# Once-used experts without room go on in the list for both halves: 29 + 46 + 29 tiles instead of 30 + 47 + 30

## Chip, cores and metric

The kernel runs on 1 core of one Trainium2 chip. The metric is the device time of one execution, in microseconds; a time of a kernel is the median of its runs.

## The reference, cut to what matters

One layer of a hybrid decoder trunk over 256 tokens of width 2048: a mixing part (window attention and a linear recurrence) and then PEER, a retrieval of experts by product keys. Each token takes, for each of 8 heads, the best 16 of 16,384 experts; an expert is a row of a table U and a row of a table V.

```python
s = einsum('chpd,hpkd->chpk', q, sub_keys)         # two sets of 128 key scores per head
top_s, top_i = top_k(s, 16)
cand = top_s[:, :, 0, :, None] + top_s[:, :, 1, None, :]
best_s, best_c = top_k(cand.reshape(128, 8, 256), 16)
experts = i1 * 128 + i2                            # the keys of the best 16 sums
g = softmax(best_s)
act = gelu(einsum('chkd,cd->chk', u_tab[experts], x))
out = einsum('chkd,chk->cd', v_tab[experts], g * act)
```

The output is the residual plus this sum, normalised, for 256 tokens. They are worked on in two halves of 128 tokens.

## The kernel before, in words

**Mixing, up to about 500 us.** Blocks of weights of 128 output columns come in on SyncE's queue (`load`), are split into a high and a low float32r part by ScalarE (`hi`, line 115) and VectorE (`lo`, line 117), and are multiplied with high and low parts of the activations. `items` holds all these half blocks of the first stages in one list. The loop at the end goes through them: it loads and splits block i + 1, calls block i's function, and then whatever `at` has hung on slot i.

**U, up to about 1160 us.** All 128 blocks of 128 experts of U are multiplied with all 256 tokens (`add_pair`, lines 133 and 134), so that every expert's activation for every token is known, and these are written to a table in HBM, `wg_d`, with one row of 4 x 128 numbers per expert: activations of half 0, gates of half 0, gates of half 1, activations of half 1. Beside this stage runs `routing`, a generator that `pump` advances by about 1200 ns of VectorE work per slot, always behind the `lo` of the next block. It finds the top keys and experts, has GpSimd scatter the gates into `wg_d` (256 scatters, line 701), and then calls `lists`.

**The lists.** For each half, an expert is used not at all, by one token or by several. `lists` counts this with one-hot matmuls and sorts the experts of the first 126 key columns into six classes: S0 and S1 (used by one token of this half alone), M0 and M1 (by several tokens of this half alone), DO (by one token of each half), BO (by both halves otherwise). Three lists of places are filled, each from both ends: S0 from the front and M0 from the back, DO and BO, S1 and M1. `CAPS` gives the tiles of 128 places of each class, `BASES` their first tile, `NT` their sum. Classes of one list share its room: `fits` says whether an expert's number plus those of the other end is under the room (lines 766 and 767), or under the class's cap (line 769); `cum` becomes the place. Experts that fit nowhere are counted (`many`, lines 775 and 776), summed over partitions by a matmul (line 778) and put in `nov`. At the end 128 one-hot matmuls (line 801) turn the places into a list of expert numbers, one column of 128 per tile.

**V, from about 1160 us.** `b_stage` goes over two tiles that need no list and then over the tiles of the lists in an order that spreads each class evenly, with three M1 tiles last:

```python
tail = [(M1, BASES[M1] + CAPS[M1] - 1 - i) for i in range(3)]
for k in range(6):
    n_ = CAPS[k] - (3 if k == M1 else 0)
    spread += [((j + 0.5) / n_, k, BASES[k] + j) for j in range(n_)]
order = [(BO, None)] * NLEAD2 + [(k, T_) for _, k, T_ in sorted(spread)] + tail
```

For each tile GpSimd gathers 128 rows of V (`gather_v`, line 886, 8 KB a row) and of the table (`gather_w`, line 895; a whole row for DO and BO, half of one for the others), five tiles ahead. Two tiles ahead, `split_w` makes weights out of activations and gates and `split_v` splits V's rows into `vh` (ScalarE, lines 935 and 938) and `vl` (VectorE, lines 936 and 939). Then `multiply` (line 951) adds to eight accumulators of 128x512. A tile of S0, DO or S1 has, per token half, weights that are 0 or 1, its factor being taken into the split of V; so it needs two terms per product, the others three:

```python
for tb in HALVES[k]:
    for h in range(2):
        terms = ((wh, vh), (wh, vl)) if k in ONCE else ((wh, vh), (wh, vl), (wl, vh))
        for n, (a, b) in enumerate(terms):
            for q in range(2):
                PE.matmul(box["o"][tb][2 * h + q], a[:, tb, :], b[:, 512 * q:512 * q + 512], ...)
```

Every five tiles a slice of the residual is added by an identity matmul (line 975). After the second tile `leftovers` reads `nov`; if it is over 0, a loop of 126 passes multiplies all of V's key columns with the weights of the experts that found no place. When half 0 is complete its statistics and outputs are made beside the last three tiles.

Of the kernel before, what the change touches and what calls it, by code (L numbers as in the profile page):

```python
# [9 lines left out]
F32 = mybir.dt.float32  # L10
# [5 lines left out]
ALU = mybir.AluOpType  # L16
# [29 lines left out]
NLIST = NKEY - NLEAD2  # L46
S0, M0, DO, BO, S1, M1 = range(6)
HALVES = ((0,), (0,), (0, 1), (0, 1), (1,), (1,))
CAPS = (17, 13, 13, 34, 17, 13)
BASES = (0, 17, 30, 43, 77, 94)  # L50
ONCE = (S0, DO, S1)
NT = 107
AHEAD = 5
LOOK = 2
NLEAD = 3
# [8 lines left out]
def trunk_kernel(ctx, tc, hT_d, par_d, sink_d, fg_d, win_d, wr_d, wi_d, wout_d, wq_d, sk_d, u_d, v_d, out_d):  # L64
    nc = tc.nc
    V, SC, PE, GP = nc.vector, nc.scalar, nc.tensor, nc.gpsimd
# [24 lines left out]
    def bcast(ap, shape):  # L91
        return ap.to_broadcast(shape)
# [3 lines left out]
    box = {}  # L96
# [42 lines left out]
    def aux_tile():  # L139
        return ps.tile([128, 512], F32, tag="aux", name="aux", bufs=4)  # L140
# [395 lines left out]
    def open_wq():  # L536
# [10 lines left out]
        box["id"] = idp.tile([128, 2, S], BF16, name="idT")  # L547
        box["iw"] = idp.tile([128, NT], I32, name="iw")
        box["iv"] = idp.tile([128, NT], I32, name="iv")
        box["ovf"] = idp.tile([128, NKEY], F32, name="ovf")  # L550
# [71 lines left out]
    def routing():  # L622
# [13 lines left out]
        for tb in range(2):  # L636
# [53 lines left out]
            V.tensor_copy(idT[:, :, tb * 128:tb * 128 + 128], p[:, 0:256].rearrange("p (i t) -> p i t", t=128))  # L690
            yield 1300
        yield from lists()

    def scatter(tb):
        flat = gate_v[tb].rearrange("e c -> (e c)").rearrange("(n o) -> n o", o=1)
        before = []
        for h in range(NH):
# [11 lines left out]
                mine.append(d)  # L709
            before = mine  # L710

    def lists():
        lp, idT = box["lp"], box["id"]
        iob, tri, onb = box["iob"], box["tri"], box["onb"]
# [9 lines left out]
        cl = lp.tile([128, 6, 128], BF16, name="cl", bufs=1)  # L724
        tot = lp.tile([128, 6, 128], F32, name="tot", bufs=1)
        cum = lp.tile([128, 6, 128], F32, name="cum", bufs=1)
# [16 lines left out]
        for lo_k, hi_k in ((0, 3), (3, 6)):  # L743
# [7 lines left out]
                V.tensor_tensor_scan(cum[:, k, :], ones, tot[:, k, :], 0.0, ALU.mult, ALU.add)  # L751
            pps.append((lo_k, hi_k, pp[:, :w_].rearrange("p (k c) -> p k c", c=128)))
            yield 1500
        many = lp.tile([128, 3], F32, name="many", bufs=1)
        for b, km in enumerate((M0, M1, BO)):
            V.tensor_copy(many[:, b:b + 1], cum[:, km, 127:128])
        V.tensor_tensor(cum, cum, tot, ALU.subtract)
# [4 lines left out]
        fits = tot  # L762
        for b, (ks, km) in enumerate(((S0, M0), (S1, M1), (DO, BO))):
            first = 128.0 * BASES[ks]
            end = 128.0 * (BASES[km] + CAPS[km])
            V.tensor_scalar(fits[:, ks], cum[:, ks], many[:, b:b + 1], None, ALU.add)
            V.scalar_tensor_tensor(fits[:, ks], fits[:, ks], end - first, cl[:, ks], ALU.is_lt, ALU.mult)
            V.tensor_scalar(cum[:, ks], cum[:, ks], first + 1.0, None, ALU.add)
            V.scalar_tensor_tensor(fits[:, km], cum[:, km], 128.0 * CAPS[km], cl[:, km], ALU.is_lt, ALU.mult)
            V.tensor_scalar(cum[:, km], cum[:, km], -1.0, end, ALU.mult, ALU.add)  # L770
            yield 1100
# [17 lines left out]
        yield 2200  # L789
        pl = aux_tile()[:, :2 * NT].rearrange("p (w t) -> p w t", t=NT)  # L790
        for g in range(0, NKEY, 4):
            ea = lp.tile([128, 4, 128], BF16, tag="ea", name="ea", bufs=2)
            eb = lp.tile([128, 4, NT], BF16, tag="eb", name="eb", bufs=2)
            ew = lp.tile([128, 4, 2, NT], BF16, tag="oh", name="ew", bufs=2)
            V.tensor_tensor(ea, bcast(iob[:, None, :], [128, 4, 128]), bcast(sb[:, 0, g:g + 4, None], [128, 4, 128]), ALU.is_equal)
            V.tensor_tensor(eb, bcast(iob[:, None, 0:NT], [128, 4, NT]), bcast(sb[:, 1, g:g + 4, None], [128, 4, NT]), ALU.is_equal)
            for j in range(4):
# [68 lines left out]

    tail = [(M1, BASES[M1] + CAPS[M1] - 1 - i) for i in range(3)]
    spread = []
# [4 lines that stand above are left out]
# [273 lines left out]
```

## Time and profile before

| | us |
|---|---|
| median of 3 runs | 1569.64 |
| lowest and highest run | 1564.13, 1572.21 |
| profiled execution, its time | 1567.66 |
| profiled execution, its span | 1566.0 |

In the profile, PE is TensorE's matmul, PEld its load of weights (beside matmuls), DVE VectorE, ACT ScalarE, POOL GpSimd, SP SyncE. Times are us from the start of the span unless marked ns. The ends of matmuls are modelled, so records of successive matmuls overlap: how closely they follow one another is read from their starts, or from the length of an unbroken run of them in the chain. Idle time of an engine is named with what ended it.

### The profile page before, as it was taken

Reading aid. Unit: us, or ns where it says so; the run is one execution under the profiler, and the core shown is the slowest. Engines: PE = TensorE matmul, PEld = TensorE weight load, DVE = VectorE, ACT = ScalarE, POOL = GpSimd, SP = SyncE. Lnnn points to the kernel's source line nnn. Section 1 sums busy time; section 2 is a strip of 40 time slices with the busy share of each in tenths; the row PEclk is TensorE's granted clock in tenths of the full one; section 3 lists DMA queues with packets and bytes.
Section 4 is the critical chain, followed back from the end, with each engine's and each line's share of the span. In section 5 each row is a group of like instructions: output and inputs, shape, how many; then the busy total and the mean of one; then the engine's idle time right before and its main releaser. Section 6 shows DMA issues by size and latency. Waiting matters only on the chain. (4 is left out here: it accounts for less than half of the span.)

```text
span 1566.0 us, 26985 instructions
## 1 busy us (share of the span) xinstructions
PE 1541.2 (98%) x9361; PEld 1346.6 (86%) x9361; DVE 1270.3 (81%) x2466; ACT 999.0 (64%) x1931; POOL 761.2 (49%) x539
## 2 busy tenths in 40 slices
PE   7999999999999999999999999999999999999997
PEld 6998999999988888888888888888888888887786
DVE  7878788887898998888888787555568899888896
ACT  6676675555556555555555887555567777766786
POOL 2001000000001777877787777774027677887871
PEclk9999999999999999999999999999999999999999
DMA  8997357665576888888887778888869989798895
GB/s 250 271 297 218 109 179 213 201 215 166 184 214 198 213 220 199 191 193 197 195 201 197 196 182 196 211 209 265 253 230 340 380 326 401 287 356 348 328 392 193
DMA packets 188274, 376.49 MB, mean 240 GB/s; under 512 B 51092, under 2 KB 119080, under 8 KB 173928
## 3 DMA queue, kind: packets, MB, share of 16 engines
q1 hardware_dynamic: 93432, 220.93, 46.3%
q0 software_dynamic: 59856, 136.22, 28.6%
q10 hardware_dynamic: 34848, 17.60, 3.9%
q8 instruction: 73, 1.20, 0.3%
q14 instruction: 65, 0.53, 0.1%
HBM read 336.80 MB, written 37.88 MB: 239 GB/s over the span
## 5 line engine op out<-in xcount | busy, mean ns | idle before, releaser
L133 PE MATMUL acc<-xc,hi 128*128 128x512 f32 x2048 | 730.9, 400 | 0.0
L115 ACT ACTIVATE hi<-raw 128x512 fp32r<-128x512 f32 x744 | 463.7, 629 | 385.3 <-PE acc L133 224.2
L117 DVE TENSOR_TENSOR lo<-raw,hi 128x512 fp32r<-128x512 f32 x744 | 507.5, 690 | 202.5 <-ACT hi L115 197.1
L701 POOL DMA_INDIRECT wg_d<-gw,gix x256 | 445.3, 1740 | 311.3 <-ACT hi L115 187.6
L134 PE MATMUL acc<-xc,lo 128*128 128x256 f32 x2048 | 575.1, 281 | 0.2 <-DVE lo L117 0.2
L133 PEld LDWEIGHTS acc<-xc,hi 128*128 128x128 f32 x2048 | 385.0, 188 | 88.1
L134 PEld LDWEIGHTS acc<-xc,lo 128*128 128x128 f32 x2048 | 387.1, 189 | 0.7 <-DVE lo L117 0.5
L895 POOL DMA_INDIRECT wg<-wg_d,iw x107 | 146.7, 1371 | 116.2 <-issue 111.8
L951 PE MATMUL oacc<-vl,wh 128*128 128x512 f32 x632 | 195.8, 392 | 1.2 <-DVE vl L936 0.6
L951 PE MATMUL oacc<-vh,wh 128*128 128x512 f32 x632 | 193.4, 395 | 1.5 <-ACT vh L935 0.8
L886 POOL DMA_INDIRECT vr<-v,iv x107 | 142.7, 1334 | 58.0 <-DVE vl L939 25.1
L939 DVE SCALAR_TENSOR_TENSOR vl<-vr,fac,vh 128x1024 fp32r<-128x1024 f32 x120 | 147.7, 1285 | 16.2 <-ACT vh L938 15.8
L936 DVE TENSOR_TENSOR vl<-vr,vh 128x1024 fp32r<-128x1024 f32 x124 | 147.4, 1219 | 4.3 <-ACT vh L935 4.0
L951 PEld LDWEIGHTS oacc<-vl,wh 128*128 128x128 f32 x632 | 117.6, 188 | 29.4 <-DVE vl L939 4.1
L938 ACT ACTIVATE vh<-vr,fac 128x1024 fp32r<-128x1024 f32 x120 | 129.8, 1141 | 19.2 <-DMA vr<-v,iv 13.4
L951 PEld LDWEIGHTS oacc<-vh,wh 128*128 128x128 f32 x632 | 116.4, 188 | 29.2 <-ACT vh L935 3.3
L935 ACT ACTIVATE vh<-vr 128x1024 fp32r<-128x1024 f32 x124 | 124.9, 1048 | 19.3 <-DMA vr<-v,iv 14.6
L125 PE MATMUL acc<-xgh,hi 128*128 128x256 f32 (+1 forms) x416 | 123.0, 296 | 7.4 <-ACT hi L115 6.4
L127 PE MATMUL acc<-xgh,lo 128*128 128x256 f32 (+1 forms) x416 | 119.7, 288 | 2.4 <-DVE lo L117 2.4
L951 PE MATMUL oacc<-vh,wl 128*128 128x512 f32 x392 | 120.8, 390 | 0.0
L126 PE MATMUL acc<-xgl,hi 128*128 128x256 f32 (+1 forms) x416 | 120.1, 289 | 0.3
L125 PEld LDWEIGHTS acc<-xgh,hi 128*128 128x128 f32 x416 | 79.3, 191 | 12.8 <-ACT hi L115 6.4
(289 smaller groups left out, 2134.9 us busy)
## 6 DMA issues: line engine op xcount, KB each, us to landing
raw<-u SPq DMA_DIRECT2D x256, 512.0 KB
raw<-win SPq DMA_DIRECT2D x52, 512.0 KB
wg_d<-zt SPq DMA_DIRECT2D x128, 128.0 KB
raw<-wout SPq DMA_DIRECT2D x32, 512.0 KB
raw<-wq SPq DMA_DIRECT2D x32, 512.0 KB
wg_d<-at ACTq DMA_DIRECT2D x126, 128.0 KB
wg_d<-gw,gix POOLq DMA_INDIRECT x256, 4.7
h_d<-hT POOLq DMA_DIRECT2D x4, 512.0 KB
```

The lines of the kernel that those rows point to most:

```text
L115: box["hi"] = SC.activation(hi, r, AF.Copy)
L117: box["lo"] = V.tensor_tensor(lo, r, hi.bitcast(F32), ALU.subtract)
L125: PE.matmul(acc, hi[:, c], xh[:, k0 + k, :], start=first and k == 0, stop=False)
L133: PE.matmul(acc, hi[:, c], x[:, k0 + k].rearrange("p h t -> p (h t)"), start=first and k == 0, stop=False)
L134: PE.matmul(acc[:, S:], lo[:, c], x[:, k0 + k, 0, :], start=False, stop=last and k == 7)
L701: d = GP.indirect_dma_start(out=flat, out_offset=bass.IndirectOffsetOnAxis(ap=box["ix"][:, tb, j:j + 1], axis=0), in_=box["gw"][:, tb, j:j ...
L886: GP.indirect_dma_start(out=raw, out_offset=None, in_=v_d, in_offset=bass.IndirectOffsetOnAxis(ap=box["iv"][:, T_:T_ + 1], axis=0))
L895: GP.indirect_dma_start(out=wg if k in (DO, BO) else wg[:, :256], out_offset=None, in_=wg_d, in_offset=bass.IndirectOffsetOnAxis(ap=box["i ...
L936: V.tensor_tensor(lo, r, hi.bitcast(F32), ALU.subtract)
L938: SC.activation(hi, r, AF.Copy, scale=fac)
L939: V.scalar_tensor_tensor(lo, r, fac, hi.bitcast(F32), ALU.mult, ALU.subtract)
L951: PE.matmul(box["o"][tb][2 * h + q], a[:, tb, :], b[:, 512 * q:512 * q + 512], start=tb in first and n == 0, stop=tb in stop and n == len( ...
```

## The change

Each of the three lists loses one tile: S0 and S1 have 16 and DO and BO together 46, NT is 104. An S0 or S1 expert whose number is past its own list's room gets a place in the middle list, behind the DO experts (and behind the ones that half 0 sent there), as long as the middle has places free. In DO and BO tiles both halves are multiplied, and a gate that is zero leaves the other half untouched. A new function, `spill`, works out places and fits for S0 and S1; `many` has eight columns instead of three. DO is treated as before.

```diff
--- before.py
+++ after.py
@@ -46,10 +46,10 @@
 NLIST = NKEY - NLEAD2
 S0, M0, DO, BO, S1, M1 = range(6)
 HALVES = ((0,), (0,), (0, 1), (0, 1), (1,), (1,))
-CAPS = (17, 13, 13, 34, 17, 13)
-BASES = (0, 17, 30, 43, 77, 94)
+CAPS = (16, 13, 13, 33, 16, 13)
+BASES = (0, 16, 29, 42, 75, 91)
 ONCE = (S0, DO, S1)
-NT = 107
+NT = 104
 AHEAD = 5
 LOOK = 2
 NLEAD = 3
@@ -709,6 +709,30 @@
                 mine.append(d)
             before = mine
 
+    def spill(fits, cum, cl, many, b, first, end):
+        room = end - first
+        d0 = 128.0 * BASES[DO]
+        lp = box["lp"]
+        over = lp.tile([128, 128], F32, name="over", bufs=1)
+        part = lp.tile([128, 128], F32, name="part", bufs=1)
+        if b == 0:
+            V.tensor_copy(many[:, 5:6], many[:, 4:5])
+            V.scalar_tensor_tensor(many[:, 6:7], many[:, 3:4], -room, many[:, 0:1], ALU.add, ALU.add)
+            V.tensor_scalar(many[:, 6:7], many[:, 6:7], 0.0, None, ALU.max)
+        else:
+            V.tensor_tensor(many[:, 5:6], many[:, 4:5], many[:, 6:7], ALU.add)
+        V.tensor_tensor(many[:, 7:8], many[:, 5:6], many[:, 2:3], ALU.add)
+        V.tensor_scalar(over, fits, -room, None, ALU.add)
+        V.tensor_scalar(part, over, many[:, 5:6], d0 + 1.0, ALU.add, ALU.add)
+        V.tensor_scalar(cum, cum, first + 1.0, None, ALU.add)
+        V.tensor_tensor(part, part, cum, ALU.subtract)
+        V.scalar_tensor_tensor(part, over, 0.0, part, ALU.is_ge, ALU.mult)
+        V.tensor_tensor(cum, cum, part, ALU.add)
+        V.tensor_scalar(part, over, many[:, 7:8], None, ALU.add)
+        V.scalar_tensor_tensor(part, part, 128.0 * (CAPS[DO] + CAPS[BO]), cl, ALU.is_lt, ALU.mult)
+        V.scalar_tensor_tensor(fits, over, 0.0, cl, ALU.is_lt, ALU.mult)
+        V.tensor_tensor(fits, fits, part, ALU.max)
+
     def lists():
         lp, idT = box["lp"], box["id"]
         iob, tri, onb = box["iob"], box["tri"], box["onb"]
@@ -751,7 +775,9 @@
                 V.tensor_tensor_scan(cum[:, k, :], ones, tot[:, k, :], 0.0, ALU.mult, ALU.add)
             pps.append((lo_k, hi_k, pp[:, :w_].rearrange("p (k c) -> p k c", c=128)))
             yield 1500
-        many = lp.tile([128, 3], F32, name="many", bufs=1)
+        many = lp.tile([128, 8], F32, name="many", bufs=1)
+        V.tensor_copy(many[:, 3:4], cum[:, S0, 127:128])
+        V.tensor_copy(many[:, 4:5], cum[:, DO, 127:128])
         for b, km in enumerate((M0, M1, BO)):
             V.tensor_copy(many[:, b:b + 1], cum[:, km, 127:128])
         V.tensor_tensor(cum, cum, tot, ALU.subtract)
@@ -764,8 +790,11 @@
             first = 128.0 * BASES[ks]
             end = 128.0 * (BASES[km] + CAPS[km])
             V.tensor_scalar(fits[:, ks], cum[:, ks], many[:, b:b + 1], None, ALU.add)
-            V.scalar_tensor_tensor(fits[:, ks], fits[:, ks], end - first, cl[:, ks], ALU.is_lt, ALU.mult)
-            V.tensor_scalar(cum[:, ks], cum[:, ks], first + 1.0, None, ALU.add)
+            if ks == DO:
+                V.scalar_tensor_tensor(fits[:, ks], fits[:, ks], end - first, cl[:, ks], ALU.is_lt, ALU.mult)
+                V.tensor_scalar(cum[:, ks], cum[:, ks], first + 1.0, None, ALU.add)
+            else:
+                spill(fits[:, ks], cum[:, ks], cl[:, ks], many, b, first, end)
             V.scalar_tensor_tensor(fits[:, km], cum[:, km], 128.0 * CAPS[km], cl[:, km], ALU.is_lt, ALU.mult)
             V.tensor_scalar(cum[:, km], cum[:, km], -1.0, end, ALU.mult, ALU.add)
             yield 1100
```

## Rows read from the trace of the kernel before

**Rows 1.** The page, part 2: TensorE's busy tenths in 40 slices.

```profile
PE   7999999999999999999999999999999999999997
```

**Rows 2.** Windows of the expert stage.

```profile
core 0: us, PE busy (x) PEld busy (x) DVE busy (x) ACT busy (x) POOL busy (x), PEclk, DMA share, GB/s
1165.00:1320.00 155.00, 154.85 (x699) 128.15 (x698) 138.34 (x191) 116.50 (x177) 113.67 (x88) 1.00 0.93 354
1320.00:1480.00 160.00, 158.04 (x693) 125.44 (x691) 134.29 (x178) 112.47 (x167) 126.49 (x84) 1.00 0.84 332
...
1480.00:1520.00 40.00, 40.00 (x176) 32.92 (x177) 38.56 (x55) 32.38 (x48) 30.62 (x26) 1.00 0.98 393
```

**Rows 3.** The chain that ended last: start us, us, what.

```profile
1198.33 17.24 PE oacc L951 x76
1215.57 0.45 PE oacc L975 x4
...
1544.46 1.39 ACT fin L984 x5
...
1555.68 0.98 PE oacc L951 x3
```

**Rows 4.** Line 951: duration ns min/median/max, first and last start us.

```profile
L951 PE MATMUL oacc<-vh,wh x632: 387/389/502, 1165.2 to 1554.7; 128*128 128x512 f32 x158
...
L951 PE MATMUL oacc<-vl,wh x632: 387/389/505, 1165.7 to 1556.0; 128*128 128x512 f32 x158
...
L951 PE MATMUL oacc<-vh,wl x392: 387/389/398, 1166.2 to 1556.5; 128*128 128x512 f32 x196
```

**Rows 5.** Timeline of POOL and PE: start us, us, [idle before and releaser].

```profile
1403.63 9.72 POOL L895 DMA_INDIRECT wg<-wg_d,iw  x1 [0.30 <-issue]
...
1417.47 0.73 PE L951 MATMUL oacc<-vl,wh 128*128 128x512 f32 x2 [0.28 <-DVE vl L939]
```

**Rows 6.** Groups by line and form, 1140 to 1566 us: busy us, mean ns.

```profile
L939 DVE SCALAR_TENSOR_TENSOR vl<-vr,fac,vh 128x1024 fp32r<-128x1024 f32 x120 | 147.7, 1285 | 16.2 <-ACT vh L938 15.8
L936 DVE TENSOR_TENSOR vl<-vr,vh 128x1024 fp32r<-128x1024 f32 x124 | 147.4, 1219 | 4.3 <-ACT vh L935 4.0
...
L907 DVE TENSOR_TENSOR w<-wg 128x256 f32<-128x256 f32 x47 | 19.5, 420 | 9.2 <-DMA wg<-wg_d,iw 9.2
L909 DVE TENSOR_TENSOR w<-wg 128x128 f32<-128x128 f32 x60 | 17.1, 287 | 11.4 <-DMA wg<-wg_d,iw 11.2 <-DVEq L956 0.2
L925 DVE TENSOR_TENSOR wl<-w,wh 128x256 fp32r<-128x256 f32 x36 | 15.0, 419 | 0.0
...
L918 DVE TENSOR_SCALAR wh<-wg 128x128 fp32r<-128x128 f32 x34 | 8.4, 248 | 5.4 <-PE oacc L951 5.2
```

**Rows 7.** Line 801: duration ns, first and last start us.

```profile
L801 PE MATMUL aux<-ew,ea x128: 252/257/268, 858.4 to 966.7; 128*128 128x214 bf16 x128
```

**Rows 8.** VectorE lines of the list stage: duration ns, first and last start us.

```profile
L768 DVE TENSOR_SCALAR cum<-cum x3: 218/227/469, 833.2 to 837.2; 128x128 f32<-128x128 f32 x3
...
L769 DVE SCALAR_TENSOR_TENSOR tot<-cum,cl x3: 280/284/287, 832.8 to 836.5; 128x128 f32<-128x128 f32 x3
...
L735 DVE TENSOR_TENSOR cum<-tot,F x2: 284/285/286, 812.5 to 815.3; 128x128 f32<-128x128 f32 x2
...
L756 DVE COPY many<-cum x3: 150/150/154, 827.5 to 827.6; 128x1 f32<-128x1 f32 x3
```

**Rows 9.** Timeline of VectorE and PE in the list stage.

```profile
834.75 0.69 DVE L117 TENSOR_TENSOR lo<-raw,hi 128x512 fp32r<-128x512 f32 x1 [0.43 <-ACT hi L115]
...
843.07 0.69 DVE L117 TENSOR_TENSOR lo<-raw,hi 128x512 fp32r<-128x512 f32 x1 [0.36 <-ACT hi L115]
...
846.61 0.28 DVE L776 TENSOR_REDUCE many<-ovf 128x1 f32<-128x128 f32 x1
...
846.94 0.38 PE L778 MATMUL aux<-many,ones 128*128 128x1 f32 x2 [0.29 <-DVE many L776]
```

## The prediction

> **What bounds the kernel now.** I read the page's forty slices first, then stage windows, then the chain of waits, then the lines of the last stage. The slices show TensorE at nine tenths or more from the second slice to the last but one [rows 1], so work counts only if it sits on TensorE or lets TensorE wait. The windows of the expert stage must be read beside this, because a matmul's end is modelled: TensorE has 154.85 us of 155, but VectorE has 138.34 of 155 (89%), transfers run at 0.93 of the DMA engines, and in the later window VectorE has 134.29 of 160 [rows 2]. Three resources are nearly full there. Which one leads is read from spacing: in the chain, 76 matmuls of the stage follow each other in 17.24 us [rows 3], 0.2268 us each, while a record lasts 389 ns [rows 4]. So TensorE issues without a gap at 0.2268 us. The granted clock is 1.00 in all these windows [rows 2], the upper of its two levels, 2.4 GHz.
>
> The stage holds 632 + 632 + 392 = 1656 such matmuls from 1165.2 to 1556.5 us [rows 4], 391.7 us with the last one's 0.39. Unbroken they take 1656 x 0.2268 = 375.6 us, and the residual, 16 slices of four matmuls at 0.45 us a slice [rows 3], another 7.2: 382.8. The stage therefore loses 8.9 us in all. Half of it is in the tail: the first half's statistics begin when its last matmul has ended at 1544.46, and the 36 matmuls of the last three tiles (M1, 1 half x 2 x 3 x 2 = 12 each) need 8.2 us, yet the last three begin at 1555.68 [rows 3], so the end is 4 us late. The rest lies in the middle, where one gather held POOL for 9.72 us and, 4 us after its end, TensorE waited for VectorE's split of a tile [rows 5].
>
> **Does the change do what it says?** Running the reference's own routing on its default inputs and counting experts of the first 126 key columns by class gives, for S0, M0, DO, BO, S1 and M1: 2133, 1490, 1704, 3999, 2244, 1486. The three lists hold 3623, 5703 and 3730. The new rooms are 29 x 128 = 3712, 46 x 128 = 5888 and 3712. The first list fits, the second half's list is 18 over, and the middle has 185 places free. So 18 experts move, nothing is left over, and 13,056 experts stand in 13,312 places. BO's cap (33 x 128 = 4224) and M's (1664) hold too.
>
> **Part 1, three tiles fewer.** A once-used tile of one half costs 1 half x 2 row parts x 2 terms x 2 column parts = 8 matmuls; a full tile for both halves 2 x 2 x 3 x 2 = 24. The change drops two of the former and one of the latter: 40 matmuls x 0.2268 = **9.07 us** less TensorE. This counts in full only if the other two shrink alike. VectorE loses, per once-used tile, 2 x 1.285 + 0.287 + 0.248 = 3.105 us, and for the full tile 2 x 1.219 + 0.420 + 0.419 = 3.277 [rows 6]: 9.49 us together. Transfers lose three tiles of 128 rows of 8 KB (1.049 MB each), two gate gathers of 0.131 MB and one of 0.262: 3.67 MB, at the stage's 354 GB/s [rows 2] 10.4 us. All three fall by 9 to 10.4 us, so TensorE stays first and the term is 9.07.
>
> The HBM Reference of the Trainium skill, section Specifications (TRN2), gives about 358 GB/s per core with both of a pair streaming and about 425 alone; by its lower figure transfers would cap the stage and the three tiles would be worth an estimated 3.67 MB / 358 GB/s = 10.3 us. The trace does not agree that 358 caps this core: one window runs at 393 GB/s [rows 2].
>
> The order of tiles is drawn again from the new counts, so which once-used tiles stand side by side shifts, but the mix and the last three tiles stay. The 4 us tail keeps its size: the same statistics stand ahead of the same three tiles. Of the middle stalls I change nothing; their bounds are all gone (4.9 us gained) and, if the longer gathers strike at a worse place, as much again lost. I take zero, since POOL and transfer work per matmul hardly move. POOL issues six gathers fewer; it is not full, and I count nothing.
>
> **Part 2, the list is 104 tiles wide, not 107.** Each of 128 matmuls that lay out the list streams 208 columns instead of 214 [rows 7]. At 0.2268 us per 512 columns that is 6 / 512 x 0.2268 x 128 = **0.3 us** less; bounds are 0 and 0.9 (the 257 ns record scaled). The one-hot work on VectorE and ScalarE shrinks alike, hidden. The last of these matmuls is at 966.7 [rows 7], 198 us ahead of the stage that reads the list [rows 4], so when the list ends costs nothing.
>
> **Part 3, the spill.** For each of the two halves, two instructions change place and eight of 128x128 come new: three tensor_scalar, two scalar_tensor_tensor, three tensor_tensor, 3 x 0.227 + 2 x 0.284 + 3 x 0.285 = 2.10 us [rows 8]. One-column instructions: two copies, then four for the first half and two for the second, 8 x 0.150 = 1.2 us. Together 5.4 us of VectorE. It sits where VectorE has no room: from 834.75 to 846.61 it idles 0.43 and 0.36 us [rows 9]. Its first dependent on TensorE is the matmul that sums what did not fit (L778), which already waits for L776, 0.29 us by its row [rows 9]. TensorE takes its queue in order, so what is queued behind L778 waits too: the next block's matmuls, then ScalarE's splits that need their buffers, and SyncE's loads. Upper bound: L776 comes 5.4 - 0.8 = 4.6 us later, all of it on TensorE. Lower bound: zero, because TensorE's order is not the source's order: L778 may be laid behind matmuls of the next block, and the low parts (lo) run ahead of TensorE by the depth of their buffers. I take **0.6 us** lost, nearest to the row: the summing matmul met VectorE 0.3 us late although VectorE had stood nearly idle-free for 12 us; I double it.
>
> **Sum:** -9.07 - 0.3 + 0.6 = **-8.8 us**. The profiled execution took 1567.66 us, 1.66 around its span of 1566.0, and lies 1.98 under the median; it would become 1558.9. Against the median of 1569.64 I predict 1560.9. 0.5%, about what a measurement of this kernel can tell from no change, is 7.85 us: the forecast lies just beyond it.
>
> **Rivals.** (a) *The wait takes the list stage.* L778 keeps its slot and TensorE stands 4.6 us: -9.37 + 4.6 = -4.8, 1564.9 us. For it: VectorE's two short idles and the wait already there. Against: the matmuls of L801 were placed with little waiting though VectorE feeds them as well. (b) *Transfers set the stage.* By rows, 10.4 us go rather than 9.07: -10.4 - 0.3 + 0.6 = -10.1, 1559.5 us. For: 0.93 of the DMA engines, and POOL held 9.72 us at once [rows 2, 5]. Against: the unbroken spacing of matmuls, and a window at 393 GB/s [rows 2]; so it gets a small chance. The lower figure of the HBM Reference, Specifications (TRN2), in the Trainium skill would give nearly the same time, an estimated 10.3 us in place of 10.4; the 393 GB/s speak against that figure here. (c) *Slower: leftovers.* One expert without a place starts the leftover loop inside the expert stage: 126 passes, each with a full tile's 24 matmuls, 126 x 24 x 0.2268 = 686 us at least, so 2247 us or more. It decides at 186 experts spilling into the middle where I count 18; rounding in the kernel's scores can move some experts, not 168.
>
> **Chances.** Forecast 0.60, (a) 0.20, (b) 0.15, (c) and any other loss past 7.85 us 0.05. The forecast's own spread, from stalls of the middle and runs that lie 8 us apart, straddles the 7.85 bound: 0.38 beyond, 0.22 within. With (b) faster is 0.53; with (a) no change is 0.42; slower 0.05. Range: the low end is (b) with 0.9 instead of 0.3 from part 2 and no wait, 11.3 us under the median, less 3 us for the spread of runs: 1555. The high end is (a) plus 2 us: 1567. Only (c) and the outer tails stay out.
>
> **What would show it.** Right: 616 + 616 + 384 matmuls of the stage, still 0.2268 apart, the stage near 382.6 us; 104 gathers of each kind; eight new VectorE rows of 0.2 to 0.3 us around 833 us for each half; the wait before the summing matmul under 1.5 us. (a) shows as 3 to 5 us before that matmul or before the next block's lo; (b) as a stage shortened by over 10 us with the waits for gathered rows shorter; (c) as loop matmuls near 1170 us. The forecast falls if the stage loses more than 13 us of stalls, or under 5.

## The result, and the profile after

The changed kernel takes 1555.31 us (median of 5 runs, 1553.33 to 1557.33) against 1571.6 us for the kernel before, measured beside it (median of 5, 1564.13 to 1572.21). The ratio is 0.9907, with a 95% interval of 0.9879 to 0.9936: 0.9% faster, by the ratio some 14.6 us, where 8.8 were forecast and 1560.9 us named. The time lies at the lower edge of the range of 1555 to 1567 us.

The page of the changed kernel, its header and the engines' line:

```profile
span 1551.3 us, 26879 instructions
PE 1525.8 (98%) x9321; PEld 1338.6 (86%) x9321; DVE 1264.1 (81%) x2478; ACT 991.9 (64%) x1920; POOL 760.3 (49%) x533
```

The span is 14.7 us shorter than the 1566.0 of before. TensorE has 9321 matmuls, against 9361: the 40 that were forecast. Line 951 of before is line 980 now; its three groups (duration ns min/median/max, first and last start):

```profile
L980 PE MATMUL oacc<-vh,wh x616: 387/392/501, 1162.4 to 1539.2; 128*128 128x512 f32 x154
...
L980 PE MATMUL oacc<-vl,wh x616: 388/392/505, 1162.8 to 1541.8; 128*128 128x512 f32 x154
...
L980 PE MATMUL oacc<-vh,wl x384: 388/392/398, 1163.3 to 1542.3; 128*128 128x512 f32 x192
```

616 + 616 + 384 = 1616, as forecast. The expert stage begins 2.8 us earlier than before (1162.4, not 1165.2 [rows 4]) and lasts 1542.3 + 0.4 - 1162.4 = 380.3 us, not 391.7. So 11.4 us come from the stage and most of the rest from ahead of it. Its spacing is read from the chain of the changed kernel (start us, us, what):

```profile
1195.73 17.41 PE oacc L980 x76
...
1541.50 0.99 PE oacc L980 x3
```

76 matmuls take 17.41 us, where they took 17.24 [rows 3]: 0.2290 us each, not 0.2268. That was not forecast, and costs 1616 x 0.0022 = 3.6 us. Unbroken, the stage would now be 1616 x 0.2290 + 7.2 = 377.3 us, so it loses **3.0 us**, where it lost 8.9. The windows say where (columns as in [rows 2]):

```profile
1165.00:1320.00 155.00, 154.85 (x693) 127.33 (x692) 134.20 (x184) 113.05 (x172) 111.63 (x86) 1.00 0.93 353
1320.00:1480.00 160.00, 160.00 (x717) 131.85 (x716) 145.59 (x196) 122.14 (x179) 123.61 (x90) 1.00 0.90 353
...
1400.00:1440.00 40.00, 40.00 (x180) 32.99 (x179) 38.20 (x51) 32.84 (x49) 30.89 (x24) 1.00 0.99 394
```

In the second window TensorE now starts 717 matmuls in 160 us; before it started 693 [rows 2]. Unbroken, at its faster spacing, the kernel before would start 723 there, as it does in its second trace (b_again, below). So 30 were missing, 6.8 us of work: these are the middle stalls, and they are gone. The busy share shows this badly (158.04 and 160.00 of 160), the count well. The Trainium skill says on its page Perfetto Trace Analysis, section Identifying the Most-Contended Engine: matmul busy time is a poor measure, the load of weights a better one. The trace agrees: the weight loads go from 125.44 to 131.85 us in that window. The third row has 394 GB/s, again over the 358 of the HBM Reference in the Trainium skill (section Specifications (TRN2)) and under its 425 for a core alone.

What the stage still loses stands mostly in one place, ahead of the last tile's second term. The kernel before waited there too, but less. First its line, then the changed kernel's (in brackets the idle time before an instruction, and what ended it):

```profile
1555.68 0.73 PE L951 MATMUL oacc<-vl,wh 128*128 128x512 f32 x2 [0.60 <-DVE vl L936]
```

```profile
1541.50 0.74 PE L980 MATMUL oacc<-vl,wh 128*128 128x512 f32 x2 [1.95 <-DVE vl L965]
```

The chain of the changed kernel says why: VectorE makes the low part of the last tile (L965) only behind instructions of the first half's outputs (L1026).

```profile
1538.25 2.06 DVE fin L1026 x3
1540.31 1.14 DVE vl L965
```

The same wait, 1.6 to 2.1 us, stands at the end of every trace below with 103 or 104 tiles.

Waits for gathered rows fell too. Before (stretch 1165 to 1557 us: who waited, for what, us in total, times, longest):

```profile
ACT vh L935 <- DMA vr<-v,iv: 14.6, 8, 3.8
ACT vh L938 <- DMA vr<-v,iv: 13.4, 8, 5.4
DVE w L909 <- DMA wg<-wg_d,iw: 11.2, 8, 4.8
DVE w L907 <- DMA wg<-wg_d,iw: 9.2, 7, 3.2
```

and after (1162 to 1543 us):

```profile
DVE w L936 <- DMA wg<-wg_d,iw: 8.2, 3, 4.0
ACT vh L964 <- DMA vr<-v,iv: 7.6, 7, 2.9
ACT vh L967 <- DMA vr<-v,iv: 5.3, 5, 3.0
...
DVE w L938 <- DMA wg<-wg_d,iw: 1.6, 1, 1.6
```

That is 48.4 us of waiting for gathers before and 22.7 after, although only 3 of 107 tiles went.

Ahead of the stage, three things changed. First the spill, in the groups of its lines (the first and last start of the two halves):

```profile
L725 DVE TENSOR_SCALAR over<-tot x2: 214/216/218, 832.3 to 836.5; 128x128 f32<-128x128 f32 x2
...
L728 DVE TENSOR_TENSOR part<-part,cum x2: 276/280/283, 833.1 to 837.2; 128x128 f32<-128x128 f32 x2
L729 DVE SCALAR_TENSOR_TENSOR part<-over,part x2: 277/280/283, 833.5 to 837.6; 128x128 f32<-128x128 f32 x2
```

The durations are those that were priced (0.22 to 0.28 us, [rows 8]). The summing matmul, now line 807, waits 0.70 us, longer than the 0.29 us of [rows 9]; VectorE's and TensorE's timeline around it:

```profile
848.50 0.26 DVE L805 TENSOR_REDUCE many<-ovf 128x1 f32<-128x128 f32 x1
```

```profile
848.82 0.38 PE L807 MATMUL aux<-many,ones 128*128 128x1 f32 x2 [0.70 <-DVE many L805]
```

Second, the list's matmuls have 208 columns:

```profile
L830 PE MATMUL aux<-ew,ea x128: 249/253/263, 859.2 to 966.7; 128*128 128x208 bf16 x128
```

Third, the matmuls of U run closer together once the list is made, though nothing there was changed. A window with no list work in it, before and after:

```profile
980.00:1060.00 80.00, 80.00 (x455) 69.44 (x454) 44.62 (x71) 44.06 (x86) 60.82 (x39) 1.00 0.86 213
```

```profile
980.00:1060.00 80.00, 80.00 (x464) 70.53 (x463) 45.29 (x72) 44.70 (x88) 59.33 (x37) 1.00 0.86 214
```

464 matmuls against 455 in the same 80 us, at a granted clock of 1.00 in both, the level of 2.4 GHz: 2% more. From the same U matmul to the same U matmul (L133, counted from the first of its 2048): from number 1152 to 1280, where the spill stands, the changed kernel takes 49.9 us against 48.5; from 1280 to 1536, the list's matmuls, 98.8 against 99.9; from there to the end, with no list work, 178.5 against 181.1. So +1.4, -1.1, -2.6. The stretches before number 1152 give -0.6, and the end of the kernel -0.5.

Together: matmuls dropped -9.1, expert stage's spacing +3.6, its stalls -5.9, U's end -2.6, list matmuls -1.1, spill +1.4, the rest about -1.1: -14.8, for 14.7 in the spans.

### The profile page after: what moved, and what is told of

Read it like the earlier page. It is cut to its first block, busy times and chain, and to the rows that moved or that the text cites. A ratio compares the mean times of both kernels' runs of the same rounds, so it can differ in the third digit from the quotient of the medians.

```text
span 1551.3 us, 26879 instructions
## 1 busy us (share of the span) xinstructions
PE 1525.8 (98%) x9321; PEld 1338.6 (86%) x9321; DVE 1264.1 (81%) x2478; ACT 991.9 (64%) x1920; POOL 760.3 (49%) x533
## 4 chain that ended last, share of the span: by engine, by line
PE 95%; DVE 1%; DMA 1%; ACT 1%; issue 0%; SPq 0%; DVEq 0%; ACTq 0%
PE acc L133 30%; PE oacc L980 23%; PE acc L134 15%; PE acc L125 7%; PE acc L126 7%; PE acc L127 7%; PE aux L745 1%; PE aux L420 1%; DMA hT<-hT 1%; PE aux L830 1%; PE aux L383 1%; PE aux L320 0%; PE aux L591 0%; PE oacc L1004 0%; PE aux L417 0%
## 5 line engine op out<-in xcount | busy, mean ns | idle before, releaser
L133 PE MATMUL acc<-xc,hi 128*128 128x512 f32 x2048 | 726.4, 398 | 0.0
L701 POOL DMA_INDIRECT wg_d<-gw,gix x256 | 453.4, 1771 | 313.0 <-ACT hi L115 187.8
L133 PEld LDWEIGHTS acc<-xc,hi 128*128 128x128 f32 x2048 | 384.4, 188 | 85.0
L924 POOL DMA_INDIRECT wg<-wg_d,iw x104 | 142.5, 1370 | 102.1 <-issue 98.3
L980 PE MATMUL oacc<-vl,wh 128*128 128x512 f32 x616 | 190.4, 392 | 1.9 <-DVE vl L965 1.9
L980 PE MATMUL oacc<-vh,wh 128*128 128x512 f32 x616 | 187.4, 394 | 0.2
L915 POOL DMA_INDIRECT vr<-v,iv x104 | 137.6, 1323 | 58.8 <-issue 21.9
L968 DVE SCALAR_TENSOR_TENSOR vl<-vr,fac,vh 128x1024 fp32r<-128x1024 f32 x116 | 142.5, 1283 | 15.4 <-ACT vh L967 14.6
L965 DVE TENSOR_TENSOR vl<-vr,vh 128x1024 fp32r<-128x1024 f32 x122 | 145.1, 1218 | 6.1 <-ACT vh L964 3.8
L967 ACT ACTIVATE vh<-vr,fac 128x1024 fp32r<-128x1024 f32 x116 | 125.2, 1141 | 8.5 <-DMA vr<-v,iv 5.3
```

What stands on the lines that cost most here:

```text
L133: PE.matmul(acc, hi[:, c], x[:, k0 + k].rearrange("p h t -> p (h t)"), start=first and k == 0, stop=False)
L701: d = GP.indirect_dma_start(out=flat, out_offset=bass.IndirectOffsetOnAxis(ap=box["ix"][:, tb, j:j + 1], axis=0), in_=box["gw"][:, tb, j:j ...
L924: GP.indirect_dma_start(out=wg if k in (DO, BO) else wg[:, :256], out_offset=None, in_=wg_d, in_offset=bass.IndirectOffsetOnAxis(ap=box["i ...
L965: V.tensor_tensor(lo, r, hi.bitcast(F32), ALU.subtract)
L968: V.scalar_tensor_tensor(lo, r, fac, hi.bitcast(F32), ALU.mult, ALU.subtract)
```

## The experiments

The theory formed on these traces (A): the stalls of the stage's middle belong to the order and the number of the tiles, and the change took them along; the spill costs about 1.5 us in the list stage; the two spacings nearly cancel. Rivals: the stalls were the luck of one execution (B); the new code's layout or spacing did it, not the tiles (C).

Loss, below, is the stage's length from the rows of its matmuls less the count times the spacing and less 7.2 us, as above. It was 8.9 us before and 3.0 after.

**The two kernels again.** No edit.

> The kernel before, unchanged, for a second trace. Theory A (the stalls of the expert stage between 1380 and 1480 us belong to its order and tile count): 1564 to 1572 us, the matmuls of the stage lose again 6 to 9 us there beyond their unbroken spacing. Rival B (those stalls were the luck of one execution): the loss there is under 3 us, or in another place, and the time would then be nearer 1564. Also open: whether the spacing of the stage's matmuls (0.2268 us in the kernel before, 0.2290 in the changed one) is the same from execution to execution; if it is a property of the kernel it stays at 0.2268.

Measured: 1565.89 us (10 runs, 1561.47 to 1569.59), ratio 0.9995 [0.9976, 1.0014]. Spacing 17.24 us for 76 again. The stage lasts 393.1 us and loses 10.3, but elsewhere: its second window has no loss, and the waits stand from 1512 us on (TensorE's timeline):

```profile
1512.43 0.73 PE L951 MATMUL oacc<-vl,wh 128*128 128x512 f32 x2 [0.46 <-DVE vl L939]
1530.42 0.73 PE L951 MATMUL oacc<-vh,wh 128*128 128x512 f32 x2 [0.48 <-ACT vh L938]
...
1539.68 0.50 PE L951 MATMUL oacc<-vh,wh 128*128 128x512 f32 x1 [1.08 <-ACT vh L938]
```

The second window is unbroken here:

```profile
1320.00:1480.00 160.00, 160.00 (x723) 132.93 (x722) 143.13 (x192) 120.78 (x178) 123.98 (x86) 1.00 0.88 343
```

So the expectation that named a place was wrong, and by the place rival B's mark appeared. The size stayed: the kernel before loses 9 to 10 us in both traces, and where it does differs from one execution to the next.

> The changed kernel, unchanged, for a second trace. Theory A: 1553 to 1557 us, no loss in the middle of the expert stage, 1 to 2.5 us in its tail, about 1.1 us before the matmul that sums the leftovers. Rival B: stalls of several us appear in the middle. Spacing 0.2290 us again if it is a property of the kernel.

Measured: 1554.1 us (5 runs, 1551.17 to 1554.94), ratio 0.9913 [0.9883, 0.9943]. Spacing 0.2290 us; loss 3.3 us, at the end. For the size of the loss rival B falls: 8.9 and 10.3 on one side, 3.0 and 3.3 on the other, and three more traces with 107 tiles in the order of before, below, lose 10.2 to 16.0. The spacing belongs to the kernel, not to the execution.

**The spill alone.** The changed kernel with the rooms of before:

```diff
-CAPS = (16, 13, 13, 33, 16, 13)
-BASES = (0, 16, 29, 42, 75, 91)
-NT = 104
+CAPS = (17, 13, 13, 34, 17, 13)
+BASES = (0, 17, 30, 43, 77, 94)
+NT = 107
```

> The changed kernel with the room of before, 30 + 47 + 30 tiles: the spill's VectorE work alone, nothing dropped. Theory A: the list stage loses 1 to 1.5 us as in the changed kernel's trace and the expert stage keeps its order, its 1656 matmuls and its stalls: ratio to before 1.000 to 1.002. Rival C (what the change gains beyond its matmuls comes from the new code's layout or spacing, not from the tiles): 5 us or more faster than before, ratio under 0.997. Prediction's upper bound for the wait: 4.6 us slower, ratio 1.003.

Measured: 1569.69 us, ratio 1.0027 [1.0000, 1.0053]: slower by 4 us as the middle of an interval that reaches down to no change. The U matmuls from number 1152 to 1280 take 50.0 us, 1.5 more than before, as theory A has it; the stage loses 11.7 us, so the rest of the 4 us is of its stalls, and not settled by one trace. Spacing 0.2268 us. Rival C, which wanted it faster, falls.

**The tiles without the spill.** The kernel before with the changed kernel's `CAPS`, `BASES` and `NT`, and

```diff
-        with tc.If(n > 0):
+        with tc.If(n > 100):
```

so that 18 experts are left out.

> The kernel before with 29 + 46 + 29 tiles and no spill; the 18 experts of the second half that find no room are left out, since the loop for leftovers now starts only above 100. Theory A: the 40 matmuls and the middle stalls go and the list stage does not wait: 1 to 1.5 us faster than the changed kernel, ratio to before 0.988 to 0.991. Rival C: without the new code no more than the 9.1 us of the matmuls: ratio 0.994.

Measured: 1551.23 us, ratio 0.9904 [0.9875, 0.9932]. By the ratio this is 1.4 us under the changed kernel measured beside it, within both intervals. The trace is plainer: numbers 1152 to 1280 take 48.3 us, as before the change, and the summing matmul stands at 845.6 us:

```profile
L778 PE MATMUL aux<-many,ones x2: 250/260/271, 845.6 to 845.7; 128*128 128x1 f32 x2
```

The stage is as in the changed kernel: spacing 0.2290 us, loss 3.2. All of the gain but the spill's price thus comes from the tiles, or from what they bring with them.

**Order or load?** Two kernels with 107 tiles, walked through in the changed kernel's order. The three extra tiles come first in one and last, ahead of the last three, in the other. The edit of the first:

```diff
+    extra = (S0, BO, S1)
...
-        n_ = CAPS[k] - (3 if k == M1 else 0)
+        n_ = CAPS[k] - (3 if k == M1 else 0) - (k in extra)
...
-    order = [(BO, None)] * NLEAD2 + [(k, T_) for _, k, T_ in sorted(spread)] + tail
+    order = [(BO, None)] * NLEAD2 + [(k, BASES[k] + CAPS[k] - 1) for k in extra] + [(k, T_) for _, k, T_ in sorted(spread)] + tail
```

> The kernel before with its 107 tiles, walked through in the changed kernel's order: the three extra tiles come right behind the two tiles without a list. If the middle stalls come of the order of the tiles, they go: 4 to 6 us faster, ratio 0.996 to 0.997. If they come of the load on transfers and VectorE over the stage (or of the spacing of 0.2268 us, which asks for tiles faster), they stay: ratio 0.999 to 1.001.

Measured: 1562.95 us, ratio **0.9949** [0.9930, 0.9968], with not one matmul less. The stage's first and last group:

```profile
L952 PE MATMUL oacc<-vh,wh x632: 387/389/497, 1166.1 to 1549.2; 128*128 128x512 f32 x158
...
L952 PE MATMUL oacc<-vh,wl x392: 387/389/397, 1167.0 to 1552.6; 128*128 128x512 f32 x196
```

1552.6 + 0.4 - 1166.1 = 386.9 us, at the spacing of before (unbroken 382.8): loss 4.1. The ten times lie within 4.5 us (1560.51 to 1564.99), those of the kernel before, measured beside it, within 14.3 (1563.86 to 1578.17): the spread fell with the median.

> The kernel before with its 107 tiles in the changed kernel's order, the three extra tiles (S0, S1, BO) now at the end, ahead of the last three, instead of at the front. If the new order itself spares the stalls, the expert stage loses 3 to 5 us again: ratio to before 0.994 to 0.997. If it was the three tiles at the front, or a single lucky order, the loss is 8 us or more: ratio 0.999 to 1.002.

Measured: 1565.22 us, ratio **0.9959** [0.9937, 0.9981]. The stage lasts 389.6 us and loses 6.8, between the two bounds that were named; over 4 of them fall in its last 12 us, behind the added tiles. The ratio lies where the first alternative has it. So it is the order itself, not a lucky lead: at an equal number of tiles and the same spacing it is worth 0.4 to 0.5%.

The other way round, the changed kernel with its 104 tiles in the order of before, less that order's first S0, BO and S1:

```diff
-        n_ = CAPS[k] - (3 if k == M1 else 0)
-        spread += [((j + 0.5) / n_, k, BASES[k] + j) for j in range(n_)]
+        c_ = CAPS[k] - (3 if k == M1 else 0)
+        d_ = 1 if k in (S0, BO, S1) else 0
+        spread += [((j + d_ + 0.5) / (c_ + d_), k, BASES[k] + j) for j in range(c_)]
```

> The changed kernel, its 104 tiles walked through in the order of the kernel before less its first S0, BO and S1 tiles. If the order of before makes the stalls in the middle, they come back: the expert stage loses 6 to 9 us instead of 3, ratio to before 0.994 to 0.996. If they come back only at the faster spacing of 0.2268 us, or need 107 tiles, the stage loses 3 us as in the changed kernel: ratio 0.990 to 0.992.

Measured: 1555.15 us, ratio 0.9920 [0.9898, 0.9942]. The stalls do not come back:

```profile
L981 PE MATMUL oacc<-vh,wh x616: 387/392/505, 1166.4 to 1543.7; 128*128 128x512 f32 x154
...
L981 PE MATMUL oacc<-vh,wl x384: 388/392/398, 1167.4 to 1546.7; 128*128 128x512 f32 x192
```

1546.7 + 0.4 - 1166.4 = 380.7 us: loss 3.4. The first alternative falls. The old order loses 9 to 16 us only with 107 tiles at the spacing of 0.2268 us; either another order, or 104 tiles at 0.2290, is enough to be rid of most of it. Which of the two, fewer tiles or slower spacing, does it at 104 is not separated: no kernel here had 104 tiles at 0.2268.

**What sets the spacing?** Every kernel with 103 or 104 tiles ran its stage at 0.2290 us and every one with 107 at 0.2268. Two guesses were tried on the kernel before. One: the offset in SBUF behind the index tiles.

```diff
-        box["iw"] = idp.tile([128, NT], I32, name="iw")
-        box["iv"] = idp.tile([128, NT], I32, name="iv")
+        box["iw"] = idp.tile([128, 112], I32, name="iw")[:, :NT]
+        box["iv"] = idp.tile([128, 112], I32, name="iv")[:, :NT]
```

> The kernel before with the two index tiles 112 columns wide instead of 107, so that what lies behind them in SBUF begins at the same offset within 64 bytes as in the changed kernel. If the spacing of the expert stage's matmuls comes from that offset, it goes from 0.2268 to 0.2290 us and the U stage's pair from 350 to 347 ns for some stretches, and the time moves by under 3 us. If the spacing is a state that small waits set, it stays at 0.2268 us: ratio 0.999 to 1.001.

Measured: 1570.66 us, ratio 0.9997 [0.9976, 1.0019]; 76 matmuls in 17.24 us; loss 10.2. Not this offset, within 64 bytes.

The other: the number of columns of the list's matmuls, padded by one column per half of the pair (`NL = 108` in place of `NT` for `pl`, `eb`, `ew` and `lf`):

```diff
+NL = 108
...
-        pl = aux_tile()[:, :2 * NT].rearrange("p (w t) -> p w t", t=NT)
+        pl = aux_tile()[:, :2 * NL].rearrange("p (w t) -> p w t", t=NL)
```

> The kernel before with its list matmuls streaming 216 columns instead of 214 (two padding columns, read by nobody); all else, the 107 tiles and their order too, as before. All kernels with 208 columns so far showed a pair of U matmuls at 347 ns from these matmuls on and the expert stage at 0.2290 us, all kernels with 214 columns 350 ns and 0.2268 us. If the column count sets the spacing (216 and 208 are both multiples of 8), this one shows 347 ns and 0.2290 us: the U stage 3 to 4 us shorter, the expert stage 3.7 us longer less what it no longer stalls, 0 to 4 us faster in all, ratio 0.997 to 1.000. If not: 350 ns, 0.2268 us, ratio 1.000.

Measured: 1571.41 us, ratio 1.0005 [0.9983, 1.0028]; still 17.24 us for 76. So 216 columns do not bring the 0.2290 us. That fewer columns would is not excluded: it stands at 206 and 208 and not at 214 and 216, and no kernel with 107 tiles had as few. The stage lost 16.0 us in this trace, the most of all. What sets its spacing stays open.

U is another matter. With 216 columns it reached the faster pace in the window shown above, where the six other traces with 107 tiles have 454 or 455 matmuls:

```profile
980.00:1060.00 80.00, 80.00 (x464) 69.94 (x463) 45.44 (x73) 45.34 (x88) 62.72 (x40) 1.00 0.88 213
```

From number 1536 to the end it took 179.2 us, 181.1 before and 178.5 in the changed kernel. So the half of the expectation on the expert stage failed, and the half on U appeared in part.

**The wait spread out.** In the changed kernel the list work rests after each spilling half:

```diff
-            yield 1100
+            yield 1100 if ks == DO else 3700
```

> The changed kernel with its spill spread: after each of the two spilling halves the list work rests for a slot, so that VectorE's 5 us do not come in one stretch. If the spill costs by the waits in the list stage, 1 to 2 us of them go: ratio to before 0.2 points or less under the changed kernel's 0.991, near 0.990, and the trace shows under 0.6 us lost between 835 and 860 us. If it costs by what follows the wait (the spacing), nothing changes.

Measured: 1554.93 us, ratio 0.9897 [0.9870, 0.9923]. Nothing over 0.3 us is lost between 835 and 860 us any more, but the wait is not gone. The summing matmul has moved back:

```profile
L807 PE MATMUL aux<-many,ones x2: 250/260/271, 862.6 to 862.7; 128*128 128x1 f32 x2
```

and its wait for VectorE there is that of the changed kernel but for a tenth (0.6 us in TensorE's row, 0.7 before the spreading). Numbers 1152 to 1280 take 47.3 us, but only because list work has gone over into 1280 to 1536, which take 100.4: 147.8 us together, against 148.7 in the changed kernel. The 0.9 us that this wins are given back at the end of U, 180.3 us against 178.5. The stage begins at 1165.2 us, later than the changed kernel's, and the median is no lower. The ratio is the 0.990 that was expected, but its interval holds those of the changed kernel's two measurements, 0.9907 and 0.9913, too. So the expectation held for the place, and for the time it can't be told: the wait was moved, and the trace shows no gain.

**Versions that beat both.** The kernel before with rooms that fit, and no spill, 29 + 45 + 30 tiles:

```diff
-CAPS = (17, 13, 13, 34, 17, 13)
-BASES = (0, 17, 30, 43, 77, 94)
-NT = 107
+CAPS = (16, 13, 13, 32, 17, 13)
+BASES = (0, 16, 29, 42, 74, 91)
+NT = 104
```

> The kernel before with 29 + 45 + 30 tiles and no spill: 104 tiles too, and every expert has a place (the lists hold 3623, 5703 and 3730, the rooms are 3712, 5760 and 3840). 56 matmuls fewer than before instead of 40, and no spill work: 16 x 0.229 = 3.7 us for the matmuls and 2 to 3 us for the spill faster than the changed kernel, ratio to before 0.986 to 0.988.

Measured: 1548.85 us, ratio **0.9866** [0.9837, 0.9894]. Spacing 0.2290, loss 4.1 us, numbers 1152 to 1280 in 48.3 us. With the same number of tiles and no line of new code it is about 6 us under the changed kernel's medians: one S1 tile more, two BO tiles fewer than before, and no spill to pay.

The spread spill with 29 + 45 + 29 (`CAPS = (16, 13, 13, 32, 16, 13)`, `NT = 103`):

> The spread spill with one more tile for both halves taken away, 29 + 45 + 29: 18 experts spill, the middle has 57 places free before and 39 after. 24 matmuls fewer than the changed kernel: 24 x 0.229 = 5.5 us faster than spread104 if the stalls stay at 3 us, ratio to before 0.986; the spacing after 206 columns is open (350 ns and 0.2268 us, if only multiples of 8 change it).

Measured: 1547.63 us, ratio 0.9875 [0.9853, 0.9898], which holds the 0.986 that was expected; spacing 0.2290, loss 3.4. It cannot be told from the version without spill. Both have little room to spare: 57 places in the middle list without spill, 39 with it, for the counts of this input.

## Why the prediction was right or wrong

**Faster by more than 0.5%: right**, at 0.53 against 0.42, and the time is inside the range. The size was short by 6 us. That the range held it is in part luck: the time is 0.3 us above the low end, 1555 us, which was worked out from rival (b) and the spread of runs, not from the forecast.

**What the change does: right.** 1616 matmuls, 104 gathers of each kind, no loop of leftovers; no expert was left over. That 18 experts moved into the middle is the prediction's count; no run shows the number. Rival (c) did not occur.

**Part 1, 9.07 us: right as work, wrong as spacing.** The 40 matmuls went. The spacing that priced them was taken as fixed, and rose by 1% over all the others: 3.6 us given back. Nothing in the trace of before could show it.

**The middle stalls, taken as zero: this is the step that failed.** It read: of the middle stalls I change nothing, the order is drawn again but the mix stays. The stage's loss fell by 5.9 us, outside the stated 4.9. By the starts of the matmuls, less the spacing, 1380 to 1480 us lost 7.3 us before and 0.5 after; from 1520 us on 0.9 were lost before and 2.2 after. Two errors met. The order was treated as neutral because the mix is the same; two kernels with all 107 tiles show that the new order alone is worth 0.4 to 0.5%. (At 104 tiles the order is not needed: the old one loses 3.4 us there.) And half of the loss had been put into the tail by a wrong reading of [rows 3]: the first half's statistics at 1544.46 us begin when the first of its accumulators is complete, with 18 matmuls of the last full tile still to come, so 54 matmuls, 12.2 us, follow, and they reach 1556.7. The tail lost 0.9 us, not 4, and the middle 7.3, and so some 7 us were there to be won, not 4.9. The tail did not keep its size either: its wait grew from 0.60 to 1.95 us. And that the stalls stood in the middle was the luck of the execution traced: in b_again 8.0 us were lost from 1520 us on, and 0.6 between 1380 and 1480.

**Rival (b), transfers set the stage: its mark appeared, its mechanism is not shown.** The stage did shorten by over 10 us and the waits for gathers did halve. But the order kernels move every byte of before and lose 4.1 and 6.8 us instead of 9 to 16; a stage set by the rate of transfers would not have let them. Their waits for gathers fell as well, from 48.4 us to 39.3 and 26.2. What TensorE waits for is a late tile now and then, in a stage where VectorE and the transfers have a tenth to spare (145.59 us of 160, and 0.90).

**Part 2, 0.3 us: too low.** The stretch with the list's matmuls fell by 1.1 us, over the bound of 0.9, and the end of U by 2.6 more, because U's pace changed. The cause is open: the padded kernel, with 107 tiles and 216 columns, has the faster pace in part of U, so the width of the list may have to do with it, but not by its columns being fewer.

**Part 3, 0.6 us: the right place, under half of the size.** The list stage lost 1.4, 1.7, 1.5 and 1.8 us in the four traces of kernels that spill in one stretch (the changed kernel twice, spill107, oldorder104), within the bounds of 0 and 4.6. Doubling the wait of before was a poor rule: 5.4 us of new work met 0.8 us of idle time and TensorE's lead hid two thirds, not nine tenths. Rival (a), which had 4.6 us, is thereby excluded.

**The criterion:** the forecast was to fall if the stage lost under 5 us. It lost 3.0. Two mis-sized terms nearly cancel (spacing in the stage, 3.6, against U with the list's matmuls, -3.7); one that does not (the stalls, -5.9) made the 6 us.

## What to carry to other kernels

Where VectorE and the transfers are near 90% beside a full TensorE, the order of the work is a term of its own: price a new order as a change, with the whole of the present stalls as the upper bound, and try the order alone before adding code. Take loss as length less count times spacing, not as busy share, and ask of a late wait how many instructions really follow it. Before making lists share their room, count whether other fixed rooms hold the data: here 29 + 45 + 30 did, without a new instruction.

## What was not expected of the hardware

Back-to-back matmuls with weights loaded between them ran at two paces, both at a granted clock of 1.00 (2.4 GHz): 0.2268 and 0.2290 us for 128x512 in the expert stage, and 455 and 464 matmuls per 80 us in U, where 512 and 256 columns alternate. The pace of the expert stage was the same in both traces of each kernel taken twice and went with the number of tiles (107, or 103 and 104); an SBUF offset, 216 columns in the list's matmuls and the order of tiles left it as it was. In U, between 980 and 1060 us, all seven traces with 103 or 104 tiles start 463 or 464 matmuls, six of the seven with 107 start 454 or 455, and the seventh, with 216 columns, 464. So the faster pace in U does not need the slower one in the expert stage. The cause of either is open.

POOL's gathers mostly take about 1 us, but 5 to 8 of some 210 in each trace take 3 to 10 us, as the 9.72 us of [rows 5]. In the changed kernel:

```profile
1359.83 1.36 POOL L924 DMA_INDIRECT wg<-wg_d,iw  x1 [0.31 <-issue]
...
1364.08 9.53 POOL L924 DMA_INDIRECT wg<-wg_d,iw  x1 [0.30 <-issue]
```

TensorE loses nothing behind this one, so a long gather alone does not make a stall. That one ahead of tiles with few matmuls does, and that the order works by this, is a guess; no run tried it.
